# Moving the output stores of a row softmax from ScalarE's DMA queue into SyncE's

## The chip, the cores and the metric

The kernel runs on one core of a Trainium2 chip. The metric is the device time of one execution in microseconds (us), lower being better. Three runs of the kernel before and one profiled execution are shown below; TensorE has no work here.

## The reference

A softmax over the last axis of a float32 tensor of 16 x 1024 x 512, that is 16384 rows of 512 numbers:

```python
def reference(x):                       # x: (16, 1024, 512) float32
    x_max = np.max(x, axis=-1, keepdims=True)
    exp_x = np.exp(x - x_max)
    return (exp_x / np.sum(exp_x, axis=-1, keepdims=True)).astype(np.float32)
```

33.55 MB are read and 33.55 MB are written, and each element is touched once by a maximum, an exponential with a sum, and a scaling.

## The kernel before, in words

The 16384 rows are cut into 8 chunks (`CHUNKS`). A chunk is 128 partitions by 16 rows (`CHUNK`) by 512 numbers, or 4096 KB: each partition holds 16 consecutive rows, 32 KB, which lie together in DRAM too. One DMA loads a chunk and one DMA stores it. SBUF holds 6 chunks at once (`PLACES`) in one tile, `held`, and everything is done in place there. So loads 0 to 5 need no free place, and loads 6 and 7 go to the places of chunks 0 and 1, and must wait until those chunks have been stored.

The compute works on groups of 8 rows per partition (`GROUP`), two groups to a chunk, 16 in all. For a group g:

- `rowmax(g)` (L88) is one VectorE reduction, 128 x 4096 to 128 x 8, which gives the negated maxima (`shift`).
- `exps(g)` (L93) is eight ScalarE activations, one for each row, with `shift` as the bias; each also accumulates the sum of its row (`sums`), which costs a second short ScalarE instruction.
- `scale(g)` (L104, L106) is one VectorE reciprocal of 128 x 8 and eight VectorE multiplications of 128 x 512.

The order of instructions on each engine is written out by hand (`manual_schedule`): the main loop calls `rowmax(g)`, `exps(g)` and then `scale(g - 1)`, so that VectorE reduces group g while it would otherwise wait for the exponentials of g - 1.

All loads (`load(k)`, L71) are issued by SyncE (SP) into SP's DMA queue, which the profile lists as q1. Load 0 is moved by `loads_at_the_head` ahead of the barrier at the start of the program. All stores (`store(k)`, L74) are issued by ScalarE, in the midst of its activations, into ScalarE's own DMA queue, which the profile lists as q10. `STORE_BEHIND` says how many groups behind the last group of a chunk its store stands in ScalarE's instruction order. Loads 6 and 7 follow loads 0 to 5 in SP's order; in the program they stand behind stores 0 and 1 (`LOAD_AFTER`), and SP waits for the landing of store 0 before it issues load 6, and for that of store 1 before load 7.

DMA instructions on an engine are issued in that engine's order. An engine that waits for a semaphore ahead of a DMA holds all DMAs behind it. Once issued, each 4096 KB transfer appears in the trace as 128 packets of 32 KB, eight on each of 16 DMA engines, and each DMA engine ends each transfer with one record of 4 bytes.

Of the kernel before, what the change touches and what calls it, by code (L numbers as in the profile page):

```python
# [1 line left out]

# [4 lines left out]

F32 = mybir.dt.float32
EXP = mybir.ActivationFunctionType.Exp
AX = mybir.AxisListType.X  # L10


CHUNK = 16
CHUNKS = 8
PLACES = 6
GROUP = 8

STORE_BEHIND = [1, 1, 1, 1, 0, 0, 0, 0]

LOAD_AFTER = {0: 6, 1: 7}  # L20


AT_HEAD = {mybir.EngineType.SP: 1}

def loads_at_the_head(nc):

    main, body = nc.main_func.blocks[0], nc.main_func.blocks[1]
    for engine, count in AT_HEAD.items():  # L30
        loads = [
            i
            for i in body.instructions
            if i.engine == engine and type(i).__name__ == "InstDMACopy"
        ][:count]
        barrier = next(
            n
            for n, i in enumerate(main.instructions)
            if i.engine == engine and type(i).__name__ == "InstDrain"
        )  # L40
        for load in loads:
            body.instructions.remove(load)
        main.instructions[barrier:barrier] = loads


@with_exitstack
def kernel(
    ctx: ExitStack,
    tc: tile.TileContext,
    x: bass.AP,  # L50
    out: bass.AP,
):
    nc = tc.nc
    nc.at_finalize(loads_at_the_head)
    P = nc.NUM_PARTITIONS

    x_rows = x.flatten_outer_dims().rearrange("(c p r) d -> c p r d", p=P, r=CHUNK)
    out_rows = out.flatten_outer_dims().rearrange("(c p r) d -> c p r d", p=P, r=CHUNK)
    n, _, _, d = x_rows.shape
    assert n == CHUNKS  # L60

    data = ctx.enter_context(tc.tile_pool(name="data", bufs=1))
    stats = ctx.enter_context(tc.tile_pool(name="stats", bufs=6))
    held = data.tile([P, PLACES * CHUNK, d], F32, name="held")

    def place(k):
        at = (k % PLACES) * CHUNK
        return held[:, at : at + CHUNK, :]

    def load(k):  # L70
        nc.sync.dma_start(out=place(k), in_=x_rows[k])  # L71

    def store(k):
        nc.scalar.dma_start(out=out_rows[k], in_=place(k))  # L74
        if k in LOAD_AFTER:
            load(LOAD_AFTER[k])

    per = CHUNK // GROUP
    groups = CHUNKS * per
    shift, sums = [None] * groups, [None] * groups  # L80

    def rows(g):
        at = (g % per) * GROUP
        return place(g // per)[:, at : at + GROUP, :]

    def rowmax(g):
        shift[g] = stats.tile([P, GROUP], F32, name="shift", tag="shift")
        nc.vector.reduce_max(out=shift[g], in_=rows(g), axis=AX, negate=True)  # L88

    def exps(g):  # L90
        sums[g] = stats.tile([P, GROUP], F32, name="sums", tag="sums")
        for r in range(GROUP):
            nc.scalar.activation(  # L93
                out=rows(g)[:, r, :],
                in_=rows(g)[:, r, :],
                func=EXP,
                bias=shift[g][:, r : r + 1],
                scale=1.0,
                accum_out=sums[g][:, r : r + 1],
            )  # L100

    def scale(g):
        recip = stats.tile([P, GROUP], F32, name="recip", tag="recip")
        nc.vector.reciprocal(out=recip, in_=sums[g])  # L104
        for r in range(GROUP):
            nc.vector.tensor_scalar_mul(  # L106
                out=rows(g)[:, r, :],
                in0=rows(g)[:, r, :],
                scalar1=recip[:, r : r + 1],
            )  # L110

    with tc.manual_schedule():
        for k in range(PLACES):
            load(k)
        stored = 0
        for g in range(groups):
            rowmax(g)
            exps(g)
            if g:
                scale(g - 1)  # L120
            if stored < CHUNKS and g > (stored + 1) * per - 1 + STORE_BEHIND[stored]:
                store(stored)
                stored += 1
        scale(groups - 1)
        while stored < CHUNKS:
            store(stored)
            stored += 1


# [1 line left out]
_INS = ['x']  # L131
_OUTS = [((16, 1024, 512), 'float32')]


# [23 lines left out]
```

## Time and profile before

| what | us |
|---|---|
| median of 3 runs | 161.43 |
| lowest and highest of them | 161.29, 161.83 |
| the profiled execution's own time | 161.69 |
| span of its instructions in the profile | 159.9 |
| VectorE (DVE) busy | 123.5 (77%) |
| ScalarE (ACT) busy | 93.2 (58%) |
| mean DMA rate over the span | 420 GB/s |

The profiled execution lies inside the range of the three runs. Its span begins with the first instruction on any engine and is 1.8 us shorter than its time; what lies outside it is start and end of the program. The profile counts DMA-issuing instructions as no busy time of an engine, and shows the queues of SP and ScalarE as "SPq" and "ACTq". The granted clock was 1.0.

### The profile page before, as it was taken

The numbers are of one execution on the slowest core, as the hardware profiler recorded it, in microseconds if no ns is written. First come the engines' busy times: TensorE is split into PE (matmuls) and PEld (weight loads), VectorE is DVE, ScalarE is ACT, GpSimd is POOL, SyncE is SP. The second block draws the span as 40 slices with busy tenths as digits, with TensorE's granted clock in tenths as the row PEclk, the third lists the DMA queues.
The fourth block names the chain that finished last, engine by engine and source line by source line (L and its number), as shares of the span: only waits on it lengthen the run. The fifth ranks groups of instructions, "written<-read, shape, count | busy, mean of one in ns | idle before, by whom it ended". The sixth has DMA issues, their size and how long they took to land.

```text
span 159.9 us, 496 instructions
## 1 busy us (share of the span) xinstructions
DVE 123.5 (77%) x160; ACT 93.2 (58%) x257; POOL 0.2 (0%) x4
## 2 busy tenths in 40 slices
DVE  0008969999999999999999999999999997620000
ACT  0003799495959585867777685959594959300000
POOL 0000000000000000000000000000000000000000
DMA  8999999999999999999999999999999999999993
GB/s 270 459 443 402 451 459 402 426 469 410 402 393 393 500 412 402 467 434 410 426 459 410 418 484 404 402 500 410 402 426 484 393 410 500 402 402 500 410 402 148
DMA packets 2307, 67.13 MB, mean 420 GB/s; under 512 B 256, under 2 KB 256, under 8 KB 256
## 3 DMA queue, kind: packets, MB, share of 16 engines
q1 hardware_dynamic: 1152, 33.55, 49.5%
q10 hardware_dynamic: 1152, 33.55, 48.6%
q14 instruction: 3, 0.02, 0.0%
HBM read 33.55 MB, written 33.55 MB: 420 GB/s over the span
## 4 chain that ended last, share of the span: by engine, by line
DMA 48%; DVE 32%; ACT 8%; issue 1%; DVEq 0%; SPq 0%; ACTq 0%
DMA held<-in_x_dram 30%; DVE shift L88 19%; DMA out_dram<-held 18%; DVE held L106 12%; ACT held L93 8%; DVE recip L104 1%; DVEq L153 0%; SPq L71 0%; ACTq L93 0%
## 5 line engine op out<-in xcount | busy, mean ns | idle before, releaser
L93 ACT ACTIVATE held<-held,shift 128x512 f32<-128x512 f32 x128 | 90.5, 708 | 31.5 <-DVE shift L88 21.3
L88 DVE TENSOR_REDUCE shift<-held 128x8 f32<-128x4096 f32 x16 | 70.5, 4415 | 12.7 <-DMA held<-in_x_dram 12.7
L106 DVE TENSOR_SCALAR held<-held,recip 128x512 f32<-128x512 f32 x128 | 52.1, 482 | 0.6
L93 ACT ACTIVATION_READ_ACCUMULATOR held<-held,shift 128x1 f32 x128 | 23.9, 187 | 0.0
L93 ACT ACT_TABLE_LOAD x1 | 1.3, 1283 | 12.6 <-DMA held<-in_x_dram 12.6
L104 DVE RECIPROCAL recip<-sums 128x8 f32<-128x8 f32 x16 | 3.1, 196 | 4.0 <-ACT held L93 4.0
L142 POOL MEMSET const-bfloat16-1.0<- 128x1 bf16 x1 | 0.1, 101 | 0.0
L142 POOL MEMSET const-uint8-127<- 128x1 uint8 x1 | 0.1, 101 | 0.0
L142 POOL MEMSET const-float32-0.0<- 128x1 f32 x1 | 0.1, 98 | 0.2 <-issue 0.2
L142 POOL MEMSET const-float32-1.0<- 128x1 f32 x1 | 0.1, 98 | 0.0
## 6 DMA issues: line engine op xcount, KB each, us to landing
held<-in_x_dram SPq DMA_DIRECT2D x8, 4096.0 KB, 35.4
out_dram<-held ACTq DMA_DIRECT2D x8, 4096.0 KB, 28.4
```

Of the source, the lines that this page charges most:

```text
L88: nc.vector.reduce_max(out=shift[g], in_=rows(g), axis=AX, negate=True)
L93: nc.scalar.activation(out=rows(g)[:, r, :], in_=rows(g)[:, r, :], func=EXP, bias=shift[g][:, r : r + 1], scale=1.0, accum_out=sums[g][:, ...
L104: nc.vector.reciprocal(out=recip, in_=sums[g])
L106: nc.vector.tensor_scalar_mul(out=rows(g)[:, r, :], in0=rows(g)[:, r, :], scalar1=recip[:, r : r + 1],)
L142: nc = _bacc.Bacc("TRN2", target_bir_lowering=False, num_devices=1)
```

## The change

SP issues all 16 transfers, and ScalarE none. The order in SP's queue is: loads 0 to 5, stores 0 and 1, load 6, store 2, load 7, stores 3 to 7. `finish(g)` now stands where `scale(g)` was called, and calls `store` right behind the `scale` of a chunk's second group, so each store is waited for by SP on VectorE's semaphore. Load 6 now stands behind store 1 in the order (it stood directly behind load 5), and load 7 behind store 2. The order of work on VectorE is the same, and ScalarE's is the same without the eight DMA instructions. The sizes and places of all transfers are the same.

```diff
-STORE_BEHIND = [1, 1, 1, 1, 0, 0, 0, 0]
-
-LOAD_AFTER = {0: 6, 1: 7}
+LOAD_BEHIND = {1: 6, 2: 7}
...
     def store(k):
-        nc.scalar.dma_start(out=out_rows[k], in_=place(k))
-        if k in LOAD_AFTER:
-            load(LOAD_AFTER[k])
+        nc.sync.dma_start(out=out_rows[k], in_=place(k))
+        if k in LOAD_BEHIND:
+            load(LOAD_BEHIND[k])
...
+    def finish(g):
+        scale(g)
+        if (g + 1) % per == 0:
+            store(g // per)
+
     with tc.manual_schedule():
         for k in range(PLACES):
             load(k)
-        stored = 0
         for g in range(groups):
             rowmax(g)
             exps(g)
             if g:
-                scale(g - 1)
-            if stored < CHUNKS and g > (stored + 1) * per - 1 + STORE_BEHIND[stored]:
-                store(stored)
-                stored += 1
-        scale(groups - 1)
-        while stored < CHUNKS:
-            store(stored)
-            stored += 1
+                finish(g - 1)
+        finish(groups - 1)
```

## The prediction, made before the changed kernel ran

> **What bounds the kernel now.** I read the page first: the slices of its second part, then the queues.
>
> ```profile
> DVE  0008969999999999999999999999999997620000
> DMA  8999999999999999999999999999999999999993
> GB/s 270 459 443 402 451 459 402 426 469 410 402 393 393 500 412 402 467 434 410 426 459 410 418 484 404 402 500 410 402 426 484 393 410 500 402 402 500 410 402 148
> q1 hardware_dynamic: 1152, 33.55, 49.5%
> q10 hardware_dynamic: 1152, 33.55, 48.6%
> ```
>
> The DMA engines are busy from the first slice to the last; VectorE, the busiest compute engine, starts in slice 4 and has ended by slice 36. The two queues together fill 98% of 16 engines' span, half each. So the bound is 67.1 MB through 16 DMA engines, and the kernel can change only by what those engines lose. The chain of waits must be read with care: it says DMA 48%, DVE 32%, because it follows semaphores, and it stops at VectorE's last multiplication at 140.7 us, although the last store lands 18 us later.
>
> The second reading is the table of busy times by window.
>
> ```profile
> 12.50:42.00 29.50, 27.90 (x32) 22.09 (x60) 0.00 (x0) 1.00 1.01 437
> 42.00:46.00 4.00, 4.00 (x2) 2.08 (x6) 0.00 (x0) 1.00 0.90 319
> 46.00:83.00 37.00, 36.82 (x51) 28.75 (x80) 0.00 (x0) 1.00 1.01 436
> 119.00:157.00 38.00, 18.96 (x30) 13.95 (x40) 0.00 (x0) 1.00 0.99 429
> 157.00:159.90 2.90, 0.00 (x0) 0.00 (x0) 0.00 (x0) 1.00 0.08 34
> ```
>
> The last column is GB/s. Loads alone in one queue (first row), both queues mixed (third) and stores alone in one queue (fourth) run at the same rate, within the coarseness of whole 32 KB packets. Only around 42 to 46 us is there a dip: there the first store joins.
>
> ```profile
> 39.88 0.38 ACTq L74 DMA_DIRECT2D out_dram<-held  x1
> ```
>
> **The packet records.** The trace has one record for each packet, and on each DMA engine a packet starts when its predecessor ends (3 to 4 ns before), so the records fall into 16 chains of 128 data packets, with no idle gap in any. The common packet takes 1.213 us, load or store. So the end of an engine is its first start + 128 x 1.213 - 0.36 (the overlaps) + the excess of its longer packets and of instruction fetches in between. Times in us:
>
> | engine | first start | excess at start | instruction fetches, with the stretched packet behind each | at the first store, 41 to 48 us | later, both queues full | end |
> |---|---|---|---|---|---|---|
> | A | 1.64 | 0.82 | none | 0.47 | 0.93 | 158.77 |
> | B | 1.67 | 0.35 | 0.66 | 0.67 | 0.43 | 158.68 |
> | C | 1.11 | 0.75 | 0.64 + 0.42 | 0.36 | 0.10 | 158.29 |
> | 13 others | 0.99 to 1.35 | 0.54 to 1.06 | none | 0.53 to 0.82 | 0 (one 0.46) | 157.27 to 157.80 |
>
> Three facts carry the forecast. Every engine lost something when the first store came in; for 14 of 16 it is a load packet begun at 42.8 to 43.3 us that took 1.75 to 2.03 us, directly ahead of the first store packet. The later losses fall on load packets while the queues alternate, nearly all on the two latest engines. And in the stretches with one queue only (12 to 41 us, and 119 to 157 us) there are next to none, also not where one transfer follows another in the queue. The kernel ends with the latest engine, A: 158.77, landing seen 0.34 later at 159.1, span end at 159.9; those tails stay.
>
> **The change, part by part.**
>
> *Eight DMA issues leave ScalarE.* They take 0.34 us each, 2.7 in sum. Price 0: the compute chain ends at 140.7 and the DMA engines at 158.8. If that cover were gone, it would be worth the one stall of 0.48 that the chain of waits shows on ScalarE at 133.0.
>
> *Eight DMA issues arrive on SP,* which does no other work, at 0.33 to 0.52 each (the loads' rows). Price 0, as long as each is issued before the queue runs dry. That must be counted, since SP now waits in order.
>
> ```profile
> SPq L71 <- DMA out_dram<-held: 80.1, 2, 61.1
> 119.22 4.42 DVE L88 TENSOR_REDUCE shift<-held 128x8 f32<-128x4096 f32 x1 [0.20 <-DMA held<-in_x_dram]
> 140.77 0.34 ACTq L74 DMA_DIRECT2D out_dram<-held  x1
> ```
>
> One transfer takes 8 x 1.21 = 9.7 us on an engine. Beginning with 1.8 us lost at the start, the one queue drains so: loads 0 to 5 by 60.0, store 0 by 69.6, store 1 by 79.3, load 6 by 89.0, store 2 by 98.7, load 7 by 108.4, stores 3 to 7 by 118.1, 127.7, 137.4, 147.1, 156.8. VectorE finishes a chunk every 15.46 us (two groups of 4.33 + 0.12 + 0.02 + 3.26 = 7.73 in the chain of waits): store 0 is ready at 34.0, store 1 at 49.4, store 2 at 64.9, then 80.3, 95.7, 111.2, 126.7, and store 7 at about 140.
>
> SP reaches load 6 with store 1 already queued, waits for store 0's landing at about 70, and issues; store 1 covers 9 us of that. Behind this wait stand store 2, load 7 and all later stores. Load 7 waits for store 1's landing at about 79.7, covered by load 6 and store 2 (19 us). Stores 3 to 7 are ready 28, 22, 16, 10 and 7 us before their turn. The nearest price for "issue to first packet" has two ends: 1.0 us (load 0, idle engines) and 3.8 to 5.4 us (store 0, issued 39.88, first packets 43.65 to 45.26, busy engines). I take the second, the nearer state; all covers are longer. Store 2 is ready at 64.9, so it holds nothing up.
>
> Loads 6 and 7 land at 89 and 108 instead of 100 and 119. Group 12 needs load 6 at 103.5 and group 14 load 7 at 118.9, so VectorE's wait of 0.20 goes, at a price of 0: store 7 becomes ready a little earlier and its queue is still full.
>
> *The second queue goes.* The loss at the first store is the one thing on the path that it touches visibly. Bounds: it stays whole (0), or goes whole (-0.36 to -0.82 by engine). I take "goes": in every later case in which a transfer was issued into a queue that already held one (loads 1 to 7, stores 1 to 7) no engine shows such a loss, and store 0 will now be issued into a queue that holds three loads. The later losses of A, B and C, 0.93, 0.43 and 0.10, I take as gone too, since they appear only while two queues alternate; bounds 0 and whole.
>
> *Five turns between load and store inside one queue* are new (load 5 to store 0, store 1 to load 6, load 6 to store 2, store 2 to load 7, load 7 to store 3). No row shows one. From below 0: between 46 and 117 us each engine turned from load to store or back 53 to 55 times, and the packets stayed at 1.213; a gain is excluded since they cannot go under the common packet. From above: 0.82 for each, the worst engine's loss at the first store. I take 0, the nearer row, as it holds for over fifty turns on each engine.
>
> The Trainium skill speaks against any gain here: "DMA: Bandwidth & Descriptors", in the section "Issuing engines are not separate DMA queues", says that DMAs from different engines run on the same 16 DMA engines and interleave, and that spreading them saves only issue time. By that rule merging the queues is worth 0, and the time would stay at 161.43. The trace agrees on the rate (437 and 436 GB/s), but shows a loss where the second queue starts, which the rule does not contain.
>
> **Sum.** With the last two loss columns gone, A ends at 158.77 - 0.47 - 0.93 = 157.4, B at 158.68 - 0.67 - 0.43 = 157.6, C at 158.29 - 0.36 - 0.10 = 157.8. The latest is C, 0.95 before A now. That is 158.95 for the span and 160.74 for the profiled execution, whose time is 0.26 above the median; from the median it is 161.43 - 0.95 = **160.5**. Which engines the fetches hit is not told by the code: with C's two on A instead, A ends at 158.4 (-0.35); with none on A, B or C, at 157.4 (-1.4). This case's own range is 160.0 to 161.1.
>
> **Rivals.** A measurement of this kernel can tell about 0.3%, 0.48 us, from no change.
>
> 1. *The first store pays anyway,* because the loss belongs to the first write and not to the queue. For it: the first load packets show a loss too (0.33 to 1.03). Against: A and C passed their first store packets at 1.213, with half the loss. Then B is last at 157.6 + 0.67 = 158.25, or -0.5: 160.9.
> 2. *Nothing moves:* the late engines lose as much, now at the turns, and the time stays at 161.4. For it: A and B start 0.3 to 0.7 late, and whatever delays them may go on.
> 3. *Slower: each turn inside the one queue drains the engine.* Place: the five turns named above. Price: 0.65, the mean loss at the first store, which is this engine's only record of a store packet met unprepared; 5 x 0.65 - 0.95 = +2.3, or 163.7. It takes the sign over from 0.19 for a turn, and is visible from 0.29. For it: in the mixed stretch the two queues could prepare packets for each other, and one queue can't. Against: the fifty free turns.
> 4. *The change doesn't do what it says:* the built instruction order has 16 DMA instructions on SP in the order named and none on ScalarE, so I give this nothing.
>
> **How the numbers follow.** The forecast gets 0.52, rival 1 0.18, rival 2 0.10, rival 3 0.20. Faster by over 0.3% (under 160.95): nine tenths of the forecast's case and half of rival 1, 0.47 + 0.09, about 0.57. Slower: rival 3, 0.20. Within: the rest, 0.23. The range runs from 159.9 (fetches on none of A, B, C, and a little) to 162.2 (rival 3 at 0.35 a turn), which leaves out most of rival 3 and little else.
>
> **What would show it.** Right: one queue with 2304 packets and about 97% share; no dip around the first store, now near 60 us; common packets of 1.213 at the five turns; the 16 ends within about 0.8 us; SP waiting for store 0 until about 70 with DMA busy in all slices; no VectorE wait at L7's reduction. Wrong: load or store packets stretched at 60, 79, 89, 99 and 108 us (rival 3), one stretch at 60 alone (rival 1), or a DMA slice below 9 after 70, which would mean that a cover failed.

## The result, and the profile after

The changed kernel is slower. The median of 22 runs is 162.76 us, against 161.69 us for 22 runs of the kernel before beside it; the ratio is 1.0057, with a 95% interval of 1.0038 to 1.0075. The prediction was 160.5 us, faster, with a range up to 162.2. The profiled execution has a span of 161.3 us, against 159.9 before.

From the page of the changed kernel, busy DMA in 40 slices, its rate, and the queues:

```profile
DMA  7999999999999999999999999999999999999990
GB/s 260 455 455 390 455 447 398 447 449 406 447 447 406 447 352 463 414 415 471 415 414 471 406 406 480 417 398 463 439 390 471 439 390 471 439 390 471 439 390 24
q1 hardware_dynamic: 2304, 67.11, 97.4%
q14 instruction: 3, 0.02, 0.0%
```

There is one queue with all 2304 packets, and the DMA engines are busy throughout: no cover failed. The dip, 319 GB/s at 42 to 46 us before, has moved to slice 15, and the last slice carries almost nothing. The next two answers, tables by window (last column GB/s), show these two places.

```profile
12.50:57.00 44.50, 42.84 (x51) 33.18 (x90) 0.00 (x0) 1.00 1.01 435
57.00:61.00 4.00, 4.00 (x2) 2.48 (x8) 0.00 (x0) 1.00 1.05 379
61.00:88.00 27.00, 26.86 (x41) 20.54 (x57) 0.00 (x0) 1.00 0.99 430
88.00:92.00 4.00, 4.00 (x2) 2.46 (x8) 0.00 (x0) 1.00 0.97 410
92.00:157.00 65.00, 45.64 (x69) 34.50 (x96) 0.00 (x0) 1.00 1.01 434
157.00:161.30 4.30, 0.00 (x0) 0.00 (x0) 0.00 (x0) 1.00 0.05 23
```

The dip is where loads 0 to 5 end and store 0 begins; a smaller one stands where load 6 ends and store 2 begins. The packet records say who pays. On each DMA engine a packet again takes 1.213 us, and the 16 ends are these:

| engine | instruction fetches | lost at load 5 to store 0 | at load 6 to store 2 | end, us |
|---|---|---|---|---|
| the latest | 34.7 and 103.9 us | 1.16 | 0.72 | 160.10 |
| the second | 59.0 us | 0.98 | 0.10 | 158.75 |
| 14 others | none | 0.24 to 1.1 | 0 to 0.18 | 157.28 to 157.97 |

So 14 engines end as before, within some tenths. One is 2.1 us behind the last of them, and the kernel waits for it. At the last turn from load to store, load 7 to store 3, the second engine lost 0.47 and the latest 0.02. What SP does is as forecast; this is the timeline of its queue:

```profile
33.94 15.80 SPq L72 DMA_DIRECT2D out_dram<-held  x2
72.02 0.34 SPq L69 DMA_DIRECT2D held<-in_x_dram  x1
72.45 0.86 SPq L72 DMA_DIRECT2D out_dram<-held  x1
81.71 0.34 SPq L69 DMA_DIRECT2D held<-in_x_dram  x1
```

Stores 0 and 1 are issued from 33.9 on. Load 6 is issued at 72.0, when store 0 has landed on the latest engine too, 2 us later than worked out and still 7 us before its turn in the queue. VectorE's wait for load 7 is gone, as its row of the timeline shows (no bracket, no idle time before it):

```profile
118.85 4.41 DVE L86 TENSOR_REDUCE shift<-held 128x8 f32<-128x4096 f32 x1
```

### The profile page after: what moved, and what is told of

Read it like the earlier page. It is cut to its first block, busy times and chain, and to the rows that moved or that the text cites. A ratio compares the mean times of both kernels' runs of the same rounds, so it can differ in the third digit from the quotient of the medians.

```text
span 161.3 us, 500 instructions
## 1 busy us (share of the span) xinstructions
DVE 123.4 (77%) x160; ACT 93.2 (58%) x257; POOL 0.2 (0%) x4
## 3 DMA queue, kind: packets, MB, share of 16 engines
q1 hardware_dynamic: 2304, 67.11, 97.4%
## 4 chain that ended last, share of the span: by engine, by line
DVE 72%; DMA 8%; ACT 7%; issue 0%; DVEq 0%; ACTq 0%
DVE shift L86 40%; DVE held L104 30%; DMA held<-in_x_dram 8%; ACT held L91 7%; DVE recip L102 1%; DVEq L149 0%; ACTq L149 0%; ACTq L91 0%
```

## The experiments

The first theory after the result was this. Each instruction fetch delays one DMA engine by about 0.64 us, and an engine that is late loses more at each turn from load to store inside the one queue; the time is that of the latest engine. The rivals were that the turns cost every engine the same, and that SP's waits in order cost the time. "Late" below means behind the median of the 16 engines, and "on time" less than 0.5 us behind it. All ratios below are against runs of the kernel before on the same chip; the experiments differ from the changed kernel unless another is named.

**Is it SP as the issuer, or the one queue?** The issuers are exchanged: stores on SP, loads on ScalarE, two queues.

```diff
-        nc.sync.dma_start(out=place(k), in_=x_rows[k])
+        nc.scalar.dma_start(out=place(k), in_=x_rows[k])
...
+            if g in LOAD_BEHIND_GROUP:          # {7: 6, 9: 7}
+                load(LOAD_BEHIND_GROUP[g])
```

> Two queues again, with the roles exchanged: all stores on SP, all loads on ScalarE (load 0 ahead of the barrier, load 6 behind the exponentials of group 7, load 7 behind those of group 9), so that stores and loads alternate packet by packet as in the kernel before while SP issues the stores and waits for them in order. Theory 'late engine' (alternation spares the late engine, one queue does not): as the kernel before, 161.3 to 162.0. Rival 'waits' (SP as the issuer of stores costs the time): as the changed kernel, 162.5 to 163.

Measured: 161.74 us, ratio 1.0002 (0.9986 to 1.0018), as the kernel before. SP as the issuer of stores, and its waits for VectorE, cost nothing. SP's waits for the landing of stores 0 and 1 are not in this kernel, since the loads stand on ScalarE. For those the packet records of the changed kernel answer: the only gap between packets on any of its 16 engines is one of about 0.2 us at the first turn, when store 0 had long been issued. So the rival "waits" falls, and the cost lies in the one queue.

**How many turns?** Two and four turns from load to store instead of three, with all transfers in SP's queue:

```diff
-LOAD_BEHIND = {1: 6, 2: 7}
+LOAD_BEHIND = {1: [6, 7]}                    # two turns: L0-5 S0 S1 L6 L7 S2-7
+LOAD_BEHIND = {0: [4, 5], 1: [6], 2: [7]}    # four: L0-3 S0 L4 L5 S1 L6 S2 L7 S3-7
```

> The changed kernel with loads 6 and 7 both behind store 1: L0-5, S0, S1, L6, L7, S2-S7, so two turns from load to store instead of three. Theory 'late engine': the late engine saves its loss at the turn from load 6 to store 2 (0.7 us), the rest stays: about 0.5 us under the changed kernel, 162.2. Rival 'turns', each at 0.65 on every engine: also 0.65 us under it, but then with long packets at the turns on all engines. Rival 'waits': load 7 now waits with only load 6 queued as cover, so nothing is won, or a gap in the DMA slices appears near 80-90 us.

> The changed kernel with store 0 moved ahead: L0-3, S0, L4, L5, S1, L6, S2, L7, S3-S7 in the one queue, four turns from load to store instead of three; the computation is whole. Theory 'late engine at turns': on-time engines pay only the first turn (0.2 to 1.0 us, now near 40 us), the engine with ScalarE's fetches pays 0.3 to 1 us at each, one turn more: 0.3 to 1.0 us above the changed kernel. Rival 'long run of loads': the first run is 4 loads instead of 6 and the loss grows with the run; under the changed kernel by some tenths.

Measured: 161.77 us with two turns, ratio 1.0005 (0.9978 to 1.0033); 163.77 us with four, ratio 1.0092 (1.0060 to 1.0124). With the changed kernel's 1.0057 for three, a turn is worth about 0.4%, 0.7 us. The intervals of two and four turns lie apart; those of three and four overlap, and so does that of the changed kernel's repeat below (1.0068). The kernel with two turns came out lower than either theory had it (162.2 or a little under). A time that grows with the turns is the answer of both theories; the packets tell them apart. With four turns the latest engine, again the one with fetches at 34.6 and 103.4 us, lost 1.31, 0.77 and 0.64 us at the first three and ended at 160.81. The 13 or 14 engines that could be followed through all packets and were not late lost 0.5 to 1.2 at the first turn, but only 0.14 and 0.07 on average at the second and third. With two turns the latest lost 1.11 and 0.34 and ended at 159.47; that execution took 162.42 us, more than its kernel's median. Tables by window of the kernel with four turns:

```profile
12.50:38.00 25.50, 23.94 (x23) 18.17 (x49) 0.00 (x0) 1.00 1.01 433
38.00:42.00 4.00, 3.96 (x10) 3.98 (x11) 0.00 (x0) 1.00 1.10 377
159.00:160.00 1.00, 0.00 (x0) 0.00 (x0) 0.00 (x0) 1.00 0.08 33
```

The dip follows the first store, to 38 to 42 us, after a run of four loads. In the last row 33 GB/s in 1 us is one packet of 32 KB: a single engine is still at work after 159. The rival "long run of loads" expected less time and a smaller loss at the first turn. The loss there was 0.95 us on average over the 16 engines after four loads, and 0.69 after six in the changed kernel, so that rival falls.

**Without fetches?** ScalarE's instructions were cut first, then VectorE's too, with the same transfers:

```diff
-        for r in range(GROUP):
-            nc.scalar.activation(
-                out=rows(g)[:, r, :], ...
+        nc.scalar.activation(
+            out=rows(g), in_=rows(g), func=EXP, bias=shift[g][:, 0:1], scale=1.0,
+        )
...
-        for r in range(GROUP):               # only in the second
-            nc.vector.tensor_scalar_mul( ...
```

> The changed kernel with one activation over 128 x 4096 for a group instead of eight with sums (ScalarE's 257 instructions become 17; row sums and seven of eight row maxima are left out, the transfers are the same). Theory 'late engine': the time after is set by the one DMA engine that carries ScalarE's two instruction fetches (34.7 and 103.9 us) and loses again at later turns from load to store because it is late. Without those fetches no engine ends later than about 158.7, the span falls from 161.3 to 159.2-159.9, the time by 1.0 to 1.8 us to about 161.0-161.7. Rival 'turns': the turns cost the same for whoever makes them; the span stays at 160.8-161.5. Rival 'waits': SP's waits in one queue cost the time; also no change.

> The changed kernel's transfers in the changed kernel's order, with so few compute instructions that no instruction fetch runs beside them: one activation of 128 x 4096 for a group; the row sums, seven of eight row maxima and the scaling are left out. Theory 'late engine': without fetches the one queue has no engine later than about 158.1, span 158.9 to 159.4, time 160.6 to 161.2, under the kernel before by 0.3 to 0.7%, which is what the prediction promised for the one queue. Rival 'the one queue itself': the time stays at 162.3 or more, with another late engine.

Measured: 161.98 us with one fetch left, ratio 1.0010 (0.9992 to 1.0028), and 161.65 us with none, ratio 0.9986 (0.9959 to 1.0013). Both take back the whole loss, within their intervals, although VectorE's work is whole in the first. Without fetches the page has a single line for the queues:

```profile
q1 hardware_dynamic: 2304, 67.11, 98.5%
```

The 16 ends lie between 157.31 and 158.35 there, and no packet begins after 158, as the tail by window shows; the changed kernel, in its repeat below, has one packet begin between 158 and 159 and one between 159 and 160. The rows without fetches:

```profile
157.00:158.00 1.00, 0.00 (x0) 0.00 (x0) 0.00 (x0) 1.00 0.23 98
158.00:159.00 1.00, 0.00 (x0) 0.00 (x0) 0.00 (x0) 1.00 0.00 0
```

The expected 160.6 to 161.2 was not reached, since the first turn still cost each engine 0.25 to 0.87 and up to 0.39 at each of the next two turns, most on those behind the median. The run with one fetch missed its expectation in another way: I had expected no late engine, but the one fetch left (at 64.6 us) made its engine late; that engine lost 0.37 and 0.83 at the later turns and ended at 159.67.

> The kernel before with the same cut in ScalarE's instructions (row sums and seven of eight row maxima left out). Theory 'late engine': in the mixed queues the two engines that start late set the end, not the one with ScalarE's fetches, so little changes: 161.2 to 161.7, 0 to 0.4 us under the kernel before, and the two cut kernels are within 0.3% of each other. Rivals 'turns' and 'waits': as before too, so that the cut changed kernel stays about 0.6% above it.

The same cut in the kernel before settles nothing on the fetches. Measured: 162.49 us, ratio 1.0069 (1.0032 to 1.0107), its runs scattered from 161.85 to 164.28; with this cut two queues were no faster than one. The shorter activations let ScalarE issue its stores earlier than in the kernel before, and five engines ended between 158.28 and 158.88. It doesn't isolate the fetches, and its expectation failed. What the fetches cost in two queues was measured by no run without them.

**More fetches, at two times.** 400 tiny memsets on GpSimd, which has nothing else to do, make three fetches early or two late:

```diff
+        for _ in range(400):
+            nc.gpsimd.memset(scratch[:, 0:1], 0.0)      # at the start, or
+                                                        # behind a copy of shift[13]
```

> The changed kernel with 400 tiny GpSimd memsets to a scratch tile from the start on (some 40 us, ended before store 0 starts near 60 us), which make instruction fetches of GpSimd run through a DMA engine while loads 1 to 4 run; nothing of the computation changes. Theory 'late engine': each fetch makes its engine 0.64 us late, and an engine that is late by about 1 to 2 us at the turns from load to store loses another 0.5 to 1.5 us there, so that it ends at 160 to 161.5 whichever it is, and the time is 0.3 to 1.5 us above the changed kernel and above the run with late memsets. Rival 'turns' and rival 'waits': only the fetches themselves count, 2 or 3 x 0.64 on one engine, the same as with late memsets.

> The same 400 memsets, but held back by a copy of the maxima of group 13, so that they run from about 108 to 150 us, when only stores are left in the queue. Theory 'late engine': the fetches cost 0.64 each and nothing is added, since no turn follows: an engine that is on time ends at 157.6 + 2 or 3 x 0.64 = 158.9 to 159.5, under the 160.1 of the latest now, so the time is that of the changed kernel within 0.3 us, if another engine than the latest carries them (if it is the latest itself, up to 1.9 us more). Rivals: the same time as with early memsets.

Measured: 163.41 us with early memsets, ratio 1.0107 (1.0088 to 1.0126). That is not clear of the changed kernel's repeat below, on the same chip: 163.40 us, ratio 1.0068 (1.0037 to 1.0099). The memsets ran until 76.6 us, not for some 40, so their third fetch fell behind the first turn. The engine with GpSimd's fetches (11.5, 33.9, 61.7 us) was 1.2 us late at the first turn, lost 1.91 there (the others that could be followed lost 0.58 to 1.08), and ended at 160.52. The time of the late kernel says nothing: 188.46 us, because its memsets ran on until 185.8. Its DMA part can be read: the two added fetches fell at 129.8 and 154.4, and the latest engine ended at 158.68. In the first window below 33 GB/s is one packet, on one engine, and belongs to the early kernel; the second is the late one's, where no packet is left.

```profile
159.00:160.00 1.00, 0.00 (x0) 0.00 (x0) 0.00 (x0) 1.00 0.08 33
```

```profile
159.00:160.00 1.00, 0.00 (x0) 0.00 (x0) 0.65 (x7) 1.00 0.00 0
```

The late kernel's DMA part is even earlier than the changed kernel's 160.10, since its engine with ScalarE's fetches lost little at the first turn (0.37). So the comparison is one execution each, and the times don't part the theory from its rivals; only the 1.91 us of the late engine speaks for it.

> The kernel before with the 400 tiny GpSimd memsets from the start on, as the changed kernel had them in the earlier run (163.41). Theory 'late engine at turns of the one queue': with two queues the fetches cost only themselves, 3 x 0.64 on one engine, which then ends at 158.8 to 159.5; time 0 to 0.7 us above the kernel before, 161.6 to 162.3. Rival 'fetches cost the same in both': 0.7 to 0.9 us above the kernel before or more, as in the one queue.

Measured, with the early memsets in the kernel before: 162.70 us, ratio 1.0039 (1.0017 to 1.0061). That is 0.6 us above the kernel before by the ratio and 0.8 by the medians, above the expected 161.6 to 162.3 and within the rival's range by the medians. In one queue the same memsets cost 0.5%, 0.8 us, or 0.4% against the repeat. The two can't be told apart, so a part of my theory is not shown: that two queues spare a late engine. The packets contradict it in part: with two queues the engine with GpSimd's fetches lost 1.1 us in many small pieces of 0.06 to 0.32 at the alternation and ended at 159.97.

**What is lost at the first store?** A tiny transfer to the output at the start, DRAM to DRAM ahead of the barrier, or from a zeroed SBUF tile behind it:

```diff
+        nc.scalar.dma_start(out=out_rows[7][:, 0, 0:16], in_=x_rows[7][:, 0, 0:16])   # or
+        nc.scalar.dma_start(out=out_rows[7][:, 0, 0:16], in_=warm)
```

> The changed kernel with one tiny copy more, 64 bytes per partition row from x to out (128 x 16 numbers, overwritten by store 7 later), issued by ScalarE ahead of the start barrier beside load 0: a first write to the output at time 0. Theory 'cold first write': the stretched load packets directly ahead of store 0 (0.23 to 0.92 us near 59 us) go, below 0.1 on engines that are on time, and the time falls by about 0.5 us. Rival 'turn': the loss belongs to the first turn from a long run of loads to a store; the packets at 59 us stay stretched by 0.3 to 0.9 and the time stays within 0.3 us of the changed kernel.

> The changed kernel with one tiny store more, 128 x 16 numbers from a zeroed SBUF tile to the output, issued by ScalarE in its own queue right behind the start barrier (overwritten by store 7 later): a first store, SBUF to DRAM, near 2 us. Theory 'the first store has a cost of its own, of reading SBUF': the stretched packets ahead of store 0 near 59 us go (below 0.1 on engines that are on time), a loss of about that size stands near 2 to 6 us instead, the time changes by less than 0.5 us. Rival 'turn after a long run of loads': they stay at 0.3 to 0.9.

Measured: 162.28 us, ratio 1.0031 (1.0001 to 1.0060), and 163.13 us, ratio 1.0091 (1.0067 to 1.0114). In both the stretched packets near 59 us stay, up to 1.3 us on an engine in the first and up to 1.05 in the second. The time of the first is about 0.4 us under the changed kernel, which is what the theory "cold first write" expected, but the two intervals overlap, and the packets decide against it. The dip stays too, first kernel, then second:

```profile
57.00:61.00 4.00, 4.00 (x2) 2.64 (x8) 0.00 (x0) 1.00 0.98 322
```

```profile
57.00:61.00 4.00, 4.00 (x2) 2.65 (x8) 0.00 (x0) 1.00 1.03 371
```

So the loss isn't that of a first small write to the output or of a first small read of SBUF. What it is stays open.

**The changed kernel once more.**

> The changed kernel once more, on the same chip as the other three, for a second look at its packets. Theory 'late engine': again the latest DMA engine is the one with ScalarE's two fetches, about 2 us behind the middle of the 16, with long load packets at the turns from loads 5, 6 or 7 to the next store and none at the turns from store to load; 162.3 to 162.9. Rival: another engine or another place in the queue.

Measured: 163.40 us, ratio 1.0068 (1.0037 to 1.0099), a little above the expected time. One engine ended at 160.49, the next at 158.48. ScalarE's fetches were at 34.5 and 104.3, and the latest engine had its long packet, 1.14 us, at the turn from load 7 to store 3. Two engines' packets coincide to the nanosecond near there, at 104.57. But each engine moves 128 data packets, eight to a transfer, and only one way of parting the two chains keeps that: the latest engine is the one with ScalarE's fetches, and it came 1.5 us late to that turn. The tail by window:

```profile
157.00:158.00 1.00, 0.00 (x0) 0.00 (x0) 0.00 (x0) 1.00 0.16 66
158.00:159.00 1.00, 0.00 (x0) 0.00 (x0) 0.00 (x0) 1.00 0.08 33
159.00:160.00 1.00, 0.00 (x0) 0.00 (x0) 0.00 (x0) 1.00 0.08 33
```

No whole kernel tried beats the kernel before: the one with two turns and the one with exchanged queues equal it within their intervals.

## Why the prediction was wrong, point by point

*The bound and the covers were right.* DMA is busy in every slice but the last. ScalarE's issues, SP's issues and its waits cost nothing, as the exchanged queues and the chains of packets show; VectorE's wait at load 7 is gone and worth nothing.

*"The second queue goes" failed.* The step took the loss at the first store to be that of a second queue coming in. It stays when there is no second queue: 0.66 us on average over the 15 engines besides the latest (0.68 over all 16 before), now at 57 to 61 us. It goes with the first turn from loads to stores. The argument for "goes", that no later transfer shows such a loss when issued into a busy queue, was true and beside the point, because no later transfer is a first store. The record of before could not part the two: the stretched packet, on 14 of 16 engines the load directly ahead of the first store, was both the last ahead of the second queue and the last ahead of a store.

*"Five turns at 0" was right for most engines and wrong for the one that counts.* The two turns from store to load are free. At the later turns from load to store the changed kernel's on-time engines lost 0.04 and 0.01 on average, the latest 0.72 at one of them. The mixed stretch of before was taken as the nearer row for that; but the turns there are between packets of two queues, and its two latest engines had lost 0.93 and 0.43 in just that stretch. Those losses were in the table, and were taken as an effect of two queues. That they were an effect of being late fits the one-queue runs, where late engines lose at the turns too, but no run shows it for two queues.

*The sum.* C was to be the latest, at 157.83, and C's counterpart, with ScalarE's two fetches, was the latest, at 160.10. The 2.27 us are: 1.16 at the first turn and 0.72 at load 6 to store 2, both taken as 0; 0.22 more at the start; 0.17 more around its fetches. The kernels with two, three and four turns, and the two with fewer fetches, show that both factors are needed for the loss in time: with two turns, or with one fetch or none, it is gone within the intervals.

*The rivals.* Rival 3 had the sign, and the cost was at turns from load to store, three of its five. It put the price on every engine and every turn, and so came to 163.7. Its reason, that two queues prepare packets for each other and one can't, is shown by no run. Rival 1 was right that the first store pays anyway, but was priced without the late engine's own extra; that the loss belongs to the first write isn't shown, and a tiny earlier write doesn't remove it. Rival 2, that late engines lose at the turns, came nearest to what the packets show, and had them lose only as much as before.

*The rule.* The Trainium skill, "DMA: Bandwidth & Descriptors", section "Issuing engines are not separate DMA queues", says that DMAs run on the same 16 DMA engines and interleave, whichever engine started them. The exchanged queues agree, at 1.0002. It would have given 0 for this change; the measurement is +0.57%, and it decides: the engines are shared, but the order of packets on them differs between one queue and two, and with three turns that had a price.

*Left open:* why a late engine loses at a turn, why the first turn costs every engine, whether two queues spare a late engine, and how much of the run-to-run spread (161.91 to 163.35) is how late the engine with the fetches happens to be.

## What to carry to other kernels

When DMA bounds a kernel, look at the end of each DMA engine and not at the mean rate: here 14 of 16 engines ended as before within some tenths, and the kernel was slower by the latest one. In a single queue put loads together and stores together, and count the turns from load to store: here two cost nothing measurable against two queues, three 0.6%, four 0.9%, with instruction fetches making one engine late. A loss that coincides with two new things (here a queue and a direction) must be priced both ways until an experiment parts them.

## What the runs showed of the hardware that I had not expected

- A compute engine's instruction fetch (one 8 KB packet, mostly 0.31 us, with the next packet stretched by 0.11 to 0.35) sits in the way of data on one DMA engine. Each engine has eight packets of every 4096 KB transfer, so that no other engine takes work off a late one. With no fetch, and with much of the compute left out, the changed order ran in 161.65 us instead of 162.76.
- At the later turns from load to store in one queue, over ten profiled executions, an engine came 0.6 to 1.9 us late 19 times, and lost 0.30 to 1.16 us each time. The engines on time lost at most 0.16 on average at any such turn. Four times an engine came over 2.4 us late, about two packets, and lost 0.02 to 0.24.
